# Attention output: the sum and its low-order half transposed together and added on VectorE, instead of folded by TensorE

## Chip, cores and metric

The kernel runs on one NeuronCore of one Trainium2 chip. The metric is the device time of one execution in microseconds (us); several runs of a program give a median. The trace is of one further, profiled execution.

## What is computed

One decoder layer over 2048 rows of width 1024 (float32). A projection feeds three groups: sparse attention (8 query heads on 2 key heads, the best 256 keys of each row chosen by an indexer), an S5 state-space scan, and attention into 256 memory rows (4 heads). Cut to what matters here:

```python
p = jax.nn.softmax(logits, axis=-1)                  # DSA attention, chosen keys
o = jnp.einsum('bqgrk,bqkgd->bqgrd', p, vg)
...
pm = jax.nn.softmax(sm, axis=-1)                     # memory attention
o_mem = jnp.einsum('bhlm,bmhd->blhd', pm, m_v)
...
cat = concat([o_att * silu(g_att), o_ssm * silu(g_ssm), o_mem * silu(g_mem)])
h = layer_norm(DN_ALPHA * x + cat @ w_out, ln_g, ln_b)
```

## The kernel before

Rows go in 16 tiles of 128. First comes the projection with the indexer's scores and the search for the 256 best keys; then attention (`attention`), 64 **units** of one row tile and one pair of heads; woven into it are the last gates, the projection and attention of the memory (`unit_mem`, 8 calls of two row tiles and 4 heads) and the scan (`stage_s5`); last the output projection and layer norm (`outputs`). Instructions are written in program order with named tiles. A scheduler then puts them into a fixed order on each engine by its own estimate, and adds semaphore waits where tiles are shared. On the chip TensorE (PE), VectorE (DVE), ScalarE (ACT) and GpSimd (POOL) each work strictly through their own order; SP issues all DMAs here, in its order too.

A unit has two parts. `att_qk` computes logits (L1116, L1117), adds the mask and takes the row maximum on VectorE (L1118), and ScalarE takes the exponential (L1123). `att_pv` transposes the weights on TensorE (L1140), splits them into a rounded part `hi` (ScalarE, L1144) and a rest `lo` (VectorE, L1145), and multiplies both with V into the sum `acc` in PSUM (L1147, L1148). V is kept as 128 columns, 64 of its rounded part beside 64 of its rest, so `acc` has 128 partitions: two halves of 64 that must still be added. That is done at the unit's end. ScalarE copies `acc` (128 x 256, two heads side by side) into `oT` (L1153). TensorE multiplies each head's 128 columns of `oT` by `ident2`, two identities of 64 stacked (L1156): this transposes and adds the halves at once, and the result `po` lies in the other half of `acc`'s bank. VectorE divides it by the softmax sum (`dn`, a reciprocal of L1151) and writes it back into `oT` (L1160), from where a DMA stores it (L1162). There is one `acc` and one `oT` buffer, so the next unit's first product (L1147) must wait until VectorE has read `po`.

`unit_mem` ends each of its 32 head-and-pair steps in the same way: `moT` (L1026), `ident2` (L1029), VectorE (L1031). A float32 product with `ident2` shows as two matmul instructions in the trace, so that both heads take four; a transpose shows as one.

Of the kernel before, what the change touches and what calls it, by code (L numbers as in the profile page):

```python
# [10 lines left out]
F32 = mybir.dt.float32  # L11
# [4 lines left out]
AF = mybir.ActivationFunctionType  # L16
OP = mybir.AluOpType
AX = mybir.AxisListType
# [69 lines left out]
class Layer:  # L88
# [82 lines left out]
    def rope(self, z, h, d, tabs, e=None):  # L171

        e = e or self.nc.gpsimd
        r = d // 4
        v = z.rearrange("p (h d) -> p h d", d=d)
        ab = self.s1.tile([128, 2, h, r], F32, name="rab", tag="o", bufs=1)
        a, b = ab[:, 0], ab[:, 1]
        cc = tabs[:, None, 0:r].broadcast_to([128, h, r])
        ss = tabs[:, None, r:2 * r].broadcast_to([128, h, r])
        e.tensor_tensor(a, v[:, :, 0:r], cc, op=OP.mult)  # L180
        e.tensor_tensor(b, v[:, :, 0:r], ss, op=OP.mult)
        hf = r // 2
        e.tensor_tensor(v[:, :, 0:hf], a[:, :, 0:hf], b[:, :, hf:r], op=OP.add)
        e.tensor_tensor(v[:, :, hf:r], a[:, :, hf:r], b[:, :, 0:hf], op=OP.add)
# [793 lines left out]
    def unit_mem(self, pp, MK, MV, sp, ps):  # L978

        nc = self.nc  # L980
        P = []
        dn = sp.tile([128, 2, 4], F32, name="mdn", bufs=2)
        for j in range(2):
            i = 2 * pp + j
            q = sp.tile([128, 256], F32, name="mq", bufs=2)
            nc.sync.dma_start(out=q, in_=self.QMD[i])
            st = sp.tile([128, 4, 2, 64], F32R, name="mst", bufs=2)
            self.split_heads(st, q)
            pt = ps.tile([128, 4, 128], F32R, name="fx", bufs=2)
            for h in range(4):  # L990
                nc.tensor.transpose(pt[:, h], st[:, h].rearrange("p a d -> p (a d)"), self.identr)
            qs = sp.tile([128, 4, 128], F32R, name="mqs", bufs=2)
            nc.scalar.activation(qs, pt.bitcast(F32), AF.Copy)
            mx = sp.tile([128, 2, 2], F32, name="mmx", bufs=2)
            p = sp.tile([128, 4, 256], F32, name="mP", bufs=4)
            for b in range(2):
                lg = ps.tile([128, 2, 256], F32, name="fx", bufs=2)
                for a in range(2):
                    nc.tensor.matmul(lg[:, a], qs[:, 2 * a + b], MK[:, a, b].rearrange("p a b -> p (a b)"),
                                     start=True, stop=False)  # L1000
                    nc.tensor.matmul(lg[:, a], qs[:, 2 * a + b], MK[:, a, 2 + b].rearrange("p a b -> p (a b)"),
                                     start=False, stop=True)
                nc.vector.tensor_reduce(mx[:, b], lg, axis=AX.X, op=OP.min)
                for a in range(2):
                    h = 2 * a + b
                    nc.scalar.activation(p[:, h], lg[:, a], AF.Exp, bias=mx[:, b, a:a + 1], scale=-1.0,
                                         accum_out=dn[:, j, h:h + 1])
            P.append(p)
        nc.vector.reciprocal(dn, dn)
        om = sp.tile([128, 2, 4, 64], F32, name="mom", bufs=2)  # L1010
        for h in range(4):
            pt = ps.tile([128, 2, 2, 128], F32, name="fx", bufs=2)
            for k in range(2):
                for j in range(2):
                    nc.tensor.transpose(pt[:, k, j], P[j][:, h, k * 128:(k + 1) * 128], self.ident)
            hi = sp.tile([128, 2, 256], F32R, name="mhi", bufs=2)
            lo = sp.tile([128, 2, 256], F32R, name="mlo", bufs=2)
            pf = pt.rearrange("p k j q -> p k (j q)")
            nc.scalar.activation(hi, pf, AF.Copy)
            nc.vector.tensor_tensor(lo, pf, hi.bitcast(F32), op=OP.subtract)  # L1020
            acc = ps.tile([128, 512], F32, name="fx", bufs=2)
            for k in range(2):
                nc.tensor.matmul(acc[:, 0:256], MV[:, k, h], hi[:, k], start=(k == 0), stop=False)
                nc.tensor.matmul(acc[:, 0:256], MV[:, k, h], lo[:, k], start=False, stop=(k == 1))
            oT = sp.tile([128, 256], F32, name="moT", bufs=2)
            nc.scalar.activation(oT, acc[:, 0:256], AF.Copy)  # L1026
            po = acc[:, 256:512]
            for j in range(2):
                nc.tensor.matmul(po[:, j * 64:(j + 1) * 64], oT[:, j * 128:(j + 1) * 128], self.ident2,  # L1029
                                 start=True, stop=True)  # L1030
            nc.vector.tensor_tensor(om[:, :, h], po[:, 0:128].rearrange("p (j d) -> p j d", d=64),  # L1031
                                    dn[:, :, h:h + 1].broadcast_to([128, 2, 64]), op=OP.mult)
        for j in range(2):
            nc.sync.dma_start(out=self.OMD[2 * pp + j], in_=om[:, j].rearrange("p a b -> p (a b)"))

# [91 lines left out]
    def att_pv(self, i, pr, pd, V, sp, ps):  # L1127

        nc = self.nc
        nk = i + 1  # L1130
        g = pr // 2
        dp, P = pd[0], pd[1:]
        acc = ps.tile([128, 512], F32, name="acc", bufs=1)
        for k0 in range(0, nk, 2):
            kw = min(2, nk - k0)
            self.npt += 1
            pt = ps.tile([128, 2, 2, 128], F32, name="pt", bufs=3)
            for k in range(kw):
                for hj in range(2):
                    nc.tensor.transpose(pt[:, k, hj], P[hj][:, (k0 + k) * 128:(k0 + k + 1) * 128], self.ident)  # L1140
            hi = sp.tile([128, 2, 256], F32R, name="hi", tag=f"h{self.npt % 3}", bufs=1)
            lo = sp.tile([128, 2, 256], F32R, name="lo", tag=f"h{self.npt % 3 + 3}", bufs=1)
            pf = pt.rearrange("p k j q -> p k (j q)")
            nc.scalar.activation(hi[:, :kw], pf[:, :kw], AF.Copy)  # L1144
            nc.vector.tensor_tensor(lo[:, :kw], pf[:, :kw], hi[:, :kw].bitcast(F32), op=OP.subtract)  # L1145
            for k in range(kw):
                nc.tensor.matmul(acc[:, 0:256], V[(k0 + k) // 4][:, (k0 + k) % 4, g], hi[:, k], start=(k0 + k == 0), stop=False)  # L1147
                nc.tensor.matmul(acc[:, 0:256], V[(k0 + k) // 4][:, (k0 + k) % 4, g], lo[:, k], start=False, stop=(k0 + k == nk - 1))  # L1148
            yield
        dn = sp.tile([128, 2], F32, name="dn", bufs=2)  # L1150
        nc.vector.reciprocal(dn, dp)  # L1151
        oT = sp.tile([128, 256], F32, name="oT", tag="o", bufs=1)
        nc.scalar.activation(oT, acc[:, 0:256], AF.Copy)  # L1153
        po = acc[:, 256:512]
        for hj in range(2):
            nc.tensor.matmul(po[:, hj * 64:(hj + 1) * 64], oT[:, hj * 128:(hj + 1) * 128], self.ident2,  # L1156
                             start=True, stop=True)
        oa = oT[:, 0:128]
        ov = oa.rearrange("p (j d) -> p j d", d=64)
        nc.vector.tensor_tensor(ov, po[:, 0:128].rearrange("p (j d) -> p j d", d=64),  # L1160
                                dn[:, :, None].broadcast_to([128, 2, 64]), op=OP.mult)
        nc.sync.dma_start(out=self.OAD[i][:, pr * 128:(pr + 1) * 128], in_=oa)  # L1162

    def attention(self, K, V, sp, ps, after=None):
# [13 lines left out]
        def ahead(j):  # L1178
            i, pr = work[j]
            if pr == 0:  # L1180
                st[i] = self.att_q(i, first[i] % 2, sp)
                while kv[0] <= max(t for t, _ in work[:j + 5]):
                    self.load_kv(kv[0], K, V, sp)
                    kv[0] += 1
            pd[j] = []
            return self.att_qk(i, pr, st[i], K, sp, ps, pd[j], j % 2)
        for _ in ahead(0):
            pass
        done = 0
        for j, w in enumerate(work):  # L1190
            a, na = iter(()), 0
            if j + 1 < len(work):
                a, na = ahead(j + 1), 2 * ((work[j + 1][0] + 4) // 4)
            nb = (w[0] + 2) // 2
            k = 0
# [218 lines left out]
```

## Time and profile before

| | |
|---|---|
| median of 3 runs | 1437.96 us (1436.89 to 1439.36) |
| profiled execution, its own time | 1432.55 us |
| its span | 1430.8 us |
| TensorE busy, share of the span | 94% |
| VectorE | 74% |
| ScalarE | 61% |
| GpSimd | 36% |
| granted TensorE clock, mean | 0.977 of full speed |

The span runs from the first to the last recorded instruction; 1.75 us of the execution lie around it. Matmuls overlap each other and their ends are modelled, so TensorE's busy time says more of where it waits than of how much it could do; the distance from the start of one group of its instructions to the start of the next is the better price. Stages lie one after another in the trace: projection and search to about 600 us, then attention with memory and scan to about 1240 us, then the output projection.

### The profile page before, as it was taken

The numbers are of one execution on the slowest core, as the hardware profiler recorded it, in microseconds if no ns is written. First come the engines' busy times: TensorE is split into PE (matmuls) and PEld (weight loads), VectorE is DVE, ScalarE is ACT, GpSimd is POOL, SyncE is SP. The second block draws the span as 40 slices with busy tenths as digits, with TensorE's granted clock in tenths as the row PEclk, the third lists the DMA queues.
The fourth block names the chain that finished last, engine by engine and source line by source line (L and its number), as shares of the span: only waits on it lengthen the run. The fifth ranks groups of instructions, "written<-read, shape, count | busy, mean of one in ns | idle before, by whom it ended". The sixth has DMA issues, their size and how long they took to land. (4 is left out here: it accounts for less than half of the span.)

```text
span 1430.8 us, 25169 instructions
## 1 busy us (share of the span) xinstructions
PE 1339.1 (94%) x8398; PEld 1181.4 (83%) x8398; DVE 1056.8 (74%) x2195; ACT 877.1 (61%) x1727; POOL 512.3 (36%) x1024
## 2 busy tenths in 40 slices
PE   7898999999869999999899999999899998999997
PEld 5687888988748988998798999998788886888885
DVE  4545785599875998865788888987788789565663
ACT  4575866775646854456788888877565677422221
POOL 1778443444993010023000000008786003254441
PEclk9799999999979999999999999999999999999998
DMA  9887454446545478552423011114112015465531
GB/s 344 264 308 239 166 170 164 169 157 214 181 136 195 138 256 299 184 168 78 125 69 94 25 59 43 36 45 115 51 42 64 25 60 185 133 224 177 177 133 62
DMA packets 128714, 206.58 MB, mean 144 GB/s; under 512 B 25088, under 2 KB 81792, under 8 KB 128320
## 3 DMA queue, kind: packets, MB, share of 16 engines
q1 hardware_dynamic: 128576, 204.89, 44.0%
q8 instruction: 68, 1.11, 0.3%
q14 instruction: 70, 0.57, 0.1%
HBM read 124.00 MB, written 77.10 MB: 141 GB/s over the span
## 5 line engine op out<-in xcount | busy, mean ns | idle before, releaser
L371 PE MATMUL fx<-whi,xhi 128*128 128x256 f32 (+3 forms) x912 | 307.1, 337 | 6.2 <-ACT xhi L139 2.5
L373 PE MATMUL fx<-whi,xlo 128*128 128x256 f32 (+3 forms) x912 | 305.7, 335 | 1.6 <-DMA xlo<-XD 1.6
L372 PE MATMUL fx<-wlo,xhi 128*128 128x256 f32 (+3 forms) x912 | 305.2, 335 | 0.0
L1145 DVE TENSOR_TENSOR lo<-pt,hi 128x512 fp32r<-128x512 f32 (+1 forms) x288 | 183.3, 654 | 48.3 <-ACT hi L1144 46.4
L453 DVE SCALAR_TENSOR_TENSOR sc<-rl,wsc,sc 128x1024 f32<-128x1024 f32 (+7 forms) x154 | 172.7, 1121 | 53.0 <-ACT rl L449 48.5
L371 PEld LDWEIGHTS fx<-whi,xhi 128*128 128x128 f32 x912 | 175.5, 192 | 24.0 <-ACT xhi L139 2.9
L1144 ACT ACTIVATE hi<-pt 128x512 fp32r<-128x512 f32 (+1 forms) x288 | 157.4, 578 | 59.6 <-PE pt L1140 29.9
L373 PEld LDWEIGHTS fx<-whi,xlo 128*128 128x128 f32 x912 | 175.4, 192 | 17.1 <-DMA xlo<-XD 2.0
L372 PEld LDWEIGHTS fx<-wlo,xhi 128*128 128x128 f32 x912 | 175.5, 192 | 15.4
L1123 ACT ACTIVATE S<-S,mx 128x1024 f32<-128x1024 f32 (+15 forms) x128 | 154.4, 1209 | 41.5 <-DVE mx L1118 39.3
L1140 PE MATMUL pt<-ident,S 128*128 128x128 f32 x1088 | 169.1, 276 | 9.4 <-DVE lo L1145 5.6
L449 ACT ACTIVATE rl<-pi 128x1024 f32<-128x1024 f32 (+7 forms) x176 | 140.1, 816 | 59.7 <-PE pi L442 42.1
L1148 PE MATMUL acc<-lo,V 128*128 128x256 f32 x544 | 144.3, 293 | 3.3 <-DVE lo L1145 3.1
L1140 PEld LDWEIGHTS pt<-ident,S 128*128 128x128 f32 x1088 | 128.4, 143 | 22.3 <-DVE lo L1145 6.9
L1147 PE MATMUL acc<-hi,V 128*128 128x256 f32 x544 | 145.2, 293 | 1.8 <-ACT hi L1144 1.4
L1116 PE MATMUL pl<-K,qs 128*128 128x512 f32 x320 | 133.7, 419 | 8.7 <-DVE mx L1118 8.4
L1118 DVE CUSTOM_DVE_ANT_0 S<-pl,mb,mx 128x512 f32<-128x512 f32 (+3 forms) x192 | 123.8, 645 | 17.6 <-PE pl L1117 13.6
L1117 PE MATMUL pl<-K,qs 128*128 128x512 f32 x320 | 117.6, 368 | 0.0
L1148 PEld LDWEIGHTS acc<-lo,V 128*128 128x128 f32 x544 | 103.5, 190 | 11.3 <-DVE lo L1145 7.6
L1147 PEld LDWEIGHTS acc<-hi,V 128*128 128x128 f32 x544 | 103.6, 190 | 6.7 <-ACT hi L1144 2.1
L442 PE MATMUL pi<-kidx,qst 128*128 128x512 f32 (+3 forms) x304 | 94.8, 390 | 15.2 <-ACT rl L449 14.6
L1118 DVE CUSTOM_DVE_ANT_0 S<-pl,mb 128x512 f32<-128x512 f32 (+3 forms) x128 | 80.7, 634 | 18.3 <-PE pl L1117 10.9
(351 smaller groups left out, 2881.2 us busy)
## 6 DMA issues: line engine op xcount, KB each, us to landing
xhi<-XD SPq DMA_DIRECT2D x32, 512.0 KB, 4.1
xlo<-XD SPq DMA_DIRECT2D x32, 512.0 KB, 5.1
QD<-kt SPq DMA_DIRECT2D x32, 256.0 KB, 2.5
qs<-QD SPq DMA_DIRECT2D x32, 256.0 KB, 3.0
xo<-x SPq DMA_DIRECT2D x16, 512.0 KB, 4.4
out<-xo SPq DMA_DIRECT2D x15, 512.0 KB, 2.7
raw<-xT SPq DMA_DIRECT2D x14, 512.0 KB, 5.4
XD<-xhi SPq DMA_DIRECT2D x14, 512.0 KB, 3.3
```

What stands on the lines that cost most here:

```text
L371: nc.tensor.matmul(p, x[0][:, k], w[0][:, k], start=(k == 0), stop=False)
L372: nc.tensor.matmul(p, x[0][:, k], w[1][:, k], start=False, stop=False)
L373: nc.tensor.matmul(p, x[1][:, k], w[0][:, k], start=False, stop=(k == KT - 1))
L449: nc.scalar.activation(rl[:, :cw], pi[:, :cw], AF.Relu)
L453: nc.vector.scalar_tensor_tensor(dst, rl[:, :cw], wsc[:, h:h + 1], dst, op0=OP.mult, op1=OP.add, accum_out=stt[:, 0, ch:ch + 1] if h == 7 ...
L1118: nc.vector.tensor_tensor_reduce(S[:, c0:c0 + cw], pl[:, :cw], mb[:, c0:c0 + cw], scale=-0.125, scalar=(3e38 if ci == 0 else mx[:, ci - 1: ...
L1123: nc.scalar.activation(S[:, :n], S[:, :n], AF.Exp, bias=mx[:, nch - 1:nch], scale=-1.0, accum_out=dp[:, hj:hj + 1])
L1140: nc.tensor.transpose(pt[:, k, hj], P[hj][:, (k0 + k) * 128:(k0 + k + 1) * 128], self.ident)
L1144: nc.scalar.activation(hi[:, :kw], pf[:, :kw], AF.Copy)
L1145: nc.vector.tensor_tensor(lo[:, :kw], pf[:, :kw], hi[:, :kw].bitcast(F32), op=OP.subtract)
L1147: nc.tensor.matmul(acc[:, 0:256], V[(k0 + k) // 4][:, (k0 + k) % 4, g], hi[:, k], start=(k0 + k == 0), stop=False)
L1148: nc.tensor.matmul(acc[:, 0:256], V[(k0 + k) // 4][:, (k0 + k) % 4, g], lo[:, k], start=False, stop=(k0 + k == nk - 1))
```

## The change

Both ends, of a unit and of a memory step, are rewritten in the same way. TensorE transposes each head's 128 columns of `oT` whole (two transposes for two heads, with `ident`); the result is 128 x 256, a row's two halves of 64 side by side for each head. VectorE adds the halves with one `tensor_reduce` that reads pairs 64 apart (256 numbers in, 128 out). GpSimd multiplies by `dn` in place, and the store follows that.

In attention `po` now takes `acc`'s own columns. `accs` holds two sums of 256 columns in one PSUM bank, used by turns, and `oT` has two buffers, `o0` and `o1`, used by turns. The scratch tile of `rope` moves from the name `o` to `o0`. Lines after 1028 move down by 1 to 4.

```diff
@@ rope
-        ab = self.s1.tile([128, 2, h, r], F32, name="rab", tag="o", bufs=1)
+        ab = self.s1.tile([128, 2, h, r], F32, name="rab", tag="o0", bufs=1)
@@ unit_mem
             for j in range(2):
-                nc.tensor.matmul(po[:, j * 64:(j + 1) * 64], oT[:, j * 128:(j + 1) * 128], self.ident2,
-                                 start=True, stop=True)
-            nc.vector.tensor_tensor(om[:, :, h], po[:, 0:128].rearrange("p (j d) -> p j d", d=64),
-                                    dn[:, :, h:h + 1].broadcast_to([128, 2, 64]), op=OP.mult)
+                js = slice(j * 128, (j + 1) * 128)
+                nc.tensor.transpose(po[:, js], oT[:, js], self.ident)
+            ov = om[:, :, h]
+            nc.vector.tensor_reduce(ov, po.rearrange("p (j a d) -> p j d a", j=2, a=2), axis=AX.X, op=OP.add)
+            nc.gpsimd.tensor_tensor(ov, ov, dn[:, :, h:h + 1].broadcast_to([128, 2, 64]), op=OP.mult)
@@ att_pv
-        acc = ps.tile([128, 512], F32, name="acc", bufs=1)
+        self.npair += 1
+        acc = self.accs[:, self.npair % 2]
...
-        oT = sp.tile([128, 256], F32, name="oT", tag="o", bufs=1)
-        nc.scalar.activation(oT, acc[:, 0:256], AF.Copy)
-        po = acc[:, 256:512]
+        oT = sp.tile([128, 256], F32, name="oT", tag=self.flip("o"), bufs=1)
+        nc.scalar.activation(oT, acc, AF.Copy)
+        po = acc
         for hj in range(2):
-            nc.tensor.matmul(po[:, hj * 64:(hj + 1) * 64], oT[:, hj * 128:(hj + 1) * 128], self.ident2,
-                             start=True, stop=True)
+            hs = slice(hj * 128, (hj + 1) * 128)
+            nc.tensor.transpose(po[:, hs], oT[:, hs], self.ident)
         oa = oT[:, 0:128]
         ov = oa.rearrange("p (j d) -> p j d", d=64)
-        nc.vector.tensor_tensor(ov, po[:, 0:128].rearrange("p (j d) -> p j d", d=64),
-                                dn[:, :, None].broadcast_to([128, 2, 64]), op=OP.mult)
+        nc.vector.tensor_reduce(ov, po.rearrange("p (j a d) -> p j d a", j=2, a=2), axis=AX.X, op=OP.add)
+        nc.gpsimd.tensor_tensor(ov, ov, dn[:, :, None].broadcast_to([128, 2, 64]), op=OP.mult)
@@ attention
+        self.accs, self.npair = ps.tile([128, 2, 256], F32, name="acc", bufs=1), 0
```

The scheduler draws a new order from the first unit's end on; up to there all five engines' orders agree but for a few rows. Two places matter.

**TensorE, from the end of one attention unit (row tile 12, second pair of heads) to the first product of the next.** In these rows a bracket names the engines whose semaphore ends the wait (DVE is VectorE, Activation is ScalarE). Before:

```order
L1156 MATMUL acc<-ident_75,oT 128x64
L1116 MATMUL pl<-K,qs 128x128 [waits DVE_49]
L1117 MATMUL pl<-K,qs 128x128
L1140 MATMUL pt<-ident,S 128x128 [waits DVE_49]
L1116 MATMUL pl<-K,qs 128x512 [waits DVE_49]
L1117 MATMUL pl<-K,qs 128x512
L1140 MATMUL pt<-ident,S 128x128 x3
L1140 MATMUL pt<-ident,S 128x128 [waits DVE_49,PE_49]
L1140 MATMUL pt<-ident,S 128x128 x3
L1140 MATMUL pt<-ident,S 128x128 [waits DVE_49,PE_49]
L1140 MATMUL pt<-ident,S 128x128 x3
L1147 MATMUL acc<-hi,V 128x256 [waits DVE_49,Activation_49]
```

The same place of the change:

```order
L1159 MATMUL acc<-ident,oT 128x128
L1117 MATMUL pl<-K,qs 128x128 [waits DVE_49]
L1118 MATMUL pl<-K,qs 128x128
L1117 MATMUL pl<-K,qs 128x512 [waits DVE_49]
L1118 MATMUL pl<-K,qs 128x512
L1142 MATMUL pt<-ident,S 128x128 [waits DVE_49,PE_49]
L1142 MATMUL pt<-ident,S 128x128 x3
L1142 MATMUL pt<-ident,S 128x128 [waits DVE_49,PE_49]
L1142 MATMUL pt<-ident,S 128x128 x3
L1142 MATMUL pt<-ident,S 128x128 [waits DVE_49,PE_49]
L1142 MATMUL pt<-ident,S 128x128 x3
L1149 MATMUL acc<-hi,V 128x256 [waits DVE_49,Activation_49]
```

The unit's end and the next unit's first product stand as far apart as they did, and the first product still waits for VectorE: the instruction that releases it is now the previous unit's `tensor_reduce` (L1162), as it was the previous unit's L1160. That holds for all 63 units that follow another.

**GpSimd, in the memory attention.** Before, these are only the splits of the memory queries (L961), two by two:

```order
L961 TENSOR_TENSOR mst<-mq,mst 128x2x64 [waits DMAHW3_49,PE_49,Activation_49]
L961 TENSOR_TENSOR mst<-mq,mst 128x2x64 [waits Activation_49]
L961 TENSOR_TENSOR mst<-mq,mst 128x2x64 [waits DMAHW4_49,PE_49,Activation_49]
L961 TENSOR_TENSOR mst<-mq,mst 128x2x64 [waits Activation_49]
L961 TENSOR_TENSOR mst<-mq,mst 128x2x64 [waits DMAHW6_49,PE_49,Activation_49]
```

Now the scalings of attention (L1163) and of the memory (L1033) stand between them, each waiting for VectorE:

```order
L1163 TENSOR_TENSOR oT<-oT,dn 128x128 [waits DMAHW0_49,DVE_49]
L1033 TENSOR_TENSOR mom<-mom,mdn 128x2x64 [waits DVE_49]
L1163 TENSOR_TENSOR oT<-oT,dn 128x128 [waits DMAHW1_49,DVE_49]
L1033 TENSOR_TENSOR mom<-mom,mdn 128x2x64 [waits DVE_49] x2
L1163 TENSOR_TENSOR oT<-oT,dn 128x128 [waits DMAHW5_49,DVE_49]
L961 TENSOR_TENSOR mst<-mq,mst 128x2x64 [waits DMAHW4_49,PE_49,Activation_49]
L961 TENSOR_TENSOR mst<-mq,mst 128x2x64 [waits Activation_49]
L1033 TENSOR_TENSOR mom<-mom,mdn 128x2x64 [waits DVE_49]
```

A split, and in the scan's stage a product of the scan, now stands behind scalings that wait for a unit's end.

## Rows read from the trace of the kernel before

**Rows 1.** The page's busy time, share and instructions of each engine.

```profile
PE 1339.1 (94%) x8398; PEld 1181.4 (83%) x8398; DVE 1056.8 (74%) x2195; ACT 877.1 (61%) x1727; POOL 512.3 (36%) x1024
```

**Rows 2.** Busy time by stretch: stretch, length, each engine's busy us, granted clock, DMA.

```profile
500.00:600.00 100.00, 99.45 (x625) 89.72 (x624) 92.52 (x161) 49.18 (x67) 10.95 (x24) 1.00 0.74 245
600.00:720.00 120.00, 112.01 (x794) 100.59 (x793) 76.22 (x201) 74.77 (x186) 22.75 (x28) 1.00 0.42 132
720.00:960.00 240.00, 236.79 (x1846) 221.52 (x1844) 205.81 (x562) 198.68 (x485) 11.78 (x29) 1.00 0.17 52
960.00:1240.00 280.00, 262.08 (x1761) 229.64 (x1760) 224.38 (x481) 185.95 (x319) 126.45 (x313) 0.98 0.26 74
1240.00:1431.00 191.00, 179.70 (x854) 149.52 (x852) 112.00 (x143) 48.08 (x76) 78.06 (x78) 0.98 0.49 164
```

**Rows 3.** The same view, of L1156 alone (PE, then weight loads).

```profile
600.00:720.00 120.00, 8.86 (x60) 8.11 (x60) 1.00 0.42 132
720.00:960.00 240.00, 18.55 (x128) 17.31 (x128) 1.00 0.17 52
960.00:1240.00 280.00, 9.74 (x68) 9.40 (x68) 0.98 0.26 74
```

**Rows 4.** The same view, of L1029 alone.

```profile
720.00:960.00 240.00, 17.56 (x124) 17.02 (x124) 1.00 0.17 52
960.00:1240.00 280.00, 0.55 (x4) 0.60 (x4) 0.98 0.26 74
```

**Rows 5.** TensorE in order of time: start us, us, instruction, count.

```profile
805.84 0.60 PE L1015 MATMUL fx<-ident,mP 128*128 128x128 f32 x4
806.28 0.56 PE L1156 MATMUL acc<-ident,oT 128*128 128x64 f32 x4
806.67 0.39 PE L1140 MATMUL pt<-ident,S 128*128 128x128 f32 x2
806.90 0.56 PE L1029 MATMUL fx<-ident,moT 128*128 128x64 f32 x4
807.29 0.61 PE L1140 MATMUL pt<-ident,S 128*128 128x128 f32 x4
807.65 0.36 PE L1147 MATMUL acc<-hi,V 128*128 128x256 f32 x1
```

**Rows 6.** VectorE's groups by shape: count, busy us, mean ns, idle before and releaser.

```profile
L1145 DVE TENSOR_TENSOR lo<-pt,hi 128x512 fp32r<-128x512 f32 x256 | 171.1, 684 | 42.1 <-ACT hi L1144 41.2
L1003 DVE TENSOR_REDUCE mmx<-fx 128x2 f32<-128x512 f32 x32 | 21.7, 682 | 1.7 <-PE fx L1001 1.5
L1160 DVE TENSOR_TENSOR oT<-acc,dn 128x128 f32<-128x128 f32 x64 | 18.1, 284 | 10.0 <-PE acc L1156 8.3 <-issue 0.9 <-ACT mhi L1019 0.3
L1145 DVE TENSOR_TENSOR lo<-pt,hi 128x256 fp32r<-128x256 f32 x32 | 13.2, 416 | 6.2 <-ACT hi L1144 5.2 <-PE acc L1147 0.9
L1031 DVE TENSOR_TENSOR mom<-fx,mdn 128x128 f32<-128x128 f32 x32 | 9.0, 282 | 1.9 <-PE fx L1029 1.9
```

**Rows 7.** The same view, GpSimd's products of 128x128 and ScalarE's copy into oT.

```profile
L961 POOL TENSOR_TENSOR mst<-mq,mst 128x128 fp32r<-128x128 f32 x32 | 14.1, 462 | 207.2 <-ACT mst L960 207.2
L180 POOL TENSOR_TENSOR rab<-zs,tab 128x128 f32<-128x128 f32 x16 | 12.7, 796 | 45.9 <-ACT zs L325 45.9
L1153 ACT ACTIVATE oT<-acc 128x256 f32<-128x256 f32 x64 | 25.0, 390 | 8.1 <-PE acc L1148 4.7 <-issue 1.2 <-DMA OAD<-oT 1.2
```

**Rows 8.** Who waited for whom, 960 to 1240 us: us in total, times, longest.

```profile
POOL BP L764 <- DMA OAD<-oT: 6.5, 1, 6.5
PE pl L1116 <- DVE mx L1118: 6.4, 4, 4.1
DVE tmp L787 <- POOL BP L766: 3.4, 2, 2.5
```

**Rows 9.** The same view, 600 to 1240 us.

```profile
PEld acc L1147 <- DVE oT L1160: 1.5, 4, 0.5
```

More of the change, by code (lines that the diff above doesn't have):

```diff
@@ L1146, in att_pv @@
             for k in range(kw):
-                nc.tensor.matmul(acc[:, 0:256], V[(k0 + k) // 4][:, (k0 + k) % 4, g], hi[:, k], start=(k0 + k == 0), stop=False)
-                nc.tensor.matmul(acc[:, 0:256], V[(k0 + k) // 4][:, (k0 + k) % 4, g], lo[:, k], start=False, stop=(k0 + k == nk - 1))
+                nc.tensor.matmul(acc, V[(k0 + k) // 4][:, (k0 + k) % 4, g], hi[:, k], start=(k0 + k == 0), stop=False)
+                nc.tensor.matmul(acc, V[(k0 + k) // 4][:, (k0 + k) % 4, g], lo[:, k], start=False, stop=(k0 + k == nk - 1))
             yield
```

## The prediction

> **What bounds the kernel now.** I read the page's busy line first [rows 1]: TensorE is busy for 94% of the span and VectorE for 74%. Such shares are averages, so the second view is the busy time by stretch [rows 2], cut where the work changes. The edited instructions run only from 600 to 1240 us [rows 3, 4]; before and after that nothing is edited. In that part the reader is to see two things. TensorE has the largest number in each stretch (112 of 120, 237 of 240, 262 of 280 us), so time taken off it can shorten the kernel. And VectorE comes close behind in the long middle stretch, 205.8 of 240 us or 86%, against 64% before it and 80% after it. GpSimd is nearly free in the middle, 11.8 of 240 us, and busy for 126 of 280 us where the scan runs.
>
> **What TensorE loses and gains.** Each end of a unit or of a memory step issues four matmul instructions, and the row order shows their price as the distance to the next start: 806.28 to 806.67 and 806.90 to 807.29, 0.39 us each [rows 5]. The counts are 256 instructions at L1156 and 128 at L1029 [rows 3, 4], so 64 and 32 ends: 15 in the first stretch, 32 + 31 = 63 in the middle, 17 + 1 = 18 in the last. The two transposes that replace them are of the kind that the kernel already does. Four took 0.44 us (from 805.84) and 0.36 us (from 807.29), two took 0.23 us (from 806.67) [rows 5]. I take 0.20 us for two, with ends of 0.18 and 0.23. Each end so frees 0.39 - 0.20 = 0.19 us of TensorE (0.16 to 0.21): 96 x 0.19 = 18.2 us, by stretch 2.9, 12.0 and 3.4 us.
>
> **What VectorE gains.** It gave 284 ns and 282 ns to the product it did here, 128 numbers out of PSUM [rows 6]. Now it reduces 256 numbers to 128. No row shows a reduction into pairs. The cheap end is 284 ns, as it writes the same 128 numbers; the dear end is 682 ns, the row of the one reduction in this stage, which reads 512 numbers [rows 6]. The nearest row by size is the 256-wide subtraction out of PSUM, 416 ns, and its 512-wide form takes 684 ns, as the 512-wide reduction does, so the number of elements read seems to set the time. I take 416 ns: 0.13 us more for each end, by stretch 2.0, 8.3 and 2.4 us.
>
> **How much of the freed time counts.** In the first stretch VectorE has 76 us of work in 120, so TensorE's 2.9 us count whole. In the middle VectorE would have 205.8 + 8.3 = 214.1 us of work in 240 - 12.0 = 228 us, or 94%. The best long stretch that this trace shows, the first of [rows 2], has 92.5 us in 100; held to that, 214.1 us need 231.5 us, so 8.5 of the 12.0 us count. In the last stretch VectorE has room (227 of 277 us), but TensorE idles there for 18 us, waiting for row maxima among others [rows 8], and shorter work turns partly into longer waiting: I count half, 1.7 us. Sum: 2.9 + 8.5 + 1.7 = 13.1 us.
>
> **Edits that I cost at nothing, with their cover.**
> - Scaling on GpSimd. The nearest product of the same size took 462 ns, one in smaller pieces 796 ns [rows 7]: 96 x 0.46 = 44 us, of which 29 fall into the middle stretch, where GpSimd works 12 of 240 us. Behind a scaling stand, on its own engine, the memory splits, the scan's products and the rounding of the output weights; on SP the store of `oT`, which now waits for GpSimd in place of VectorE, and all loads ordered behind it. No DMA is added. If that cover fails it is the second rival below.
> - Two sums in a bank. The order shows that the next unit's first product waits for the previous unit's reduction, as it waited for L1160, and with the same rows in between. Nothing is freed; TensorE's weight loads waited only 1.5 us in all for that [rows 9], which is the most it could give. The Trainium skill, "PSUM — Partial Sum Buffer", section on bank collisions, says to guard PSUM by bank and not by address, since two engines may not touch one bank at once even in different columns. By that rule two sums in one bank cannot run past each other and this edit gives 0; by addresses alone it would give up to the 1.5 us of that row. The waits in the changed order agree with the rule.
> - Two `oT` buffers. ScalarE waited 1.2 us for the store of `oT` [rows 7]; it is not the bound, so I count 0 (at most 1.2 us). Its copy keeps its size and its 390 ns.
> - `rope` takes another buffer name, long before attention.
> - The chain from the last product to the next unit's first one loses 0.19 us on TensorE and gains 0.13 us on VectorE, about even.
>
> **The number.** The profiled execution took 1432.55 us, so the same execution of the change should take 1419.5 us. The median of the runs, 1437.96 us, lies 5.4 us above the profiled execution; I carry that over and predict 1425 us. A measurement of this kernel can tell about 0.2%, or 2.9 us, from no change. The scheduler's new order also moves dozens of small waits by amounts that no row shows; I let that widen the range and not move the number.
>
> **Rivals.**
> 1. *All of it counts.* VectorE runs as densely as in its best 100 us and beyond, and the waits of the last stretch shrink as well. Then 18.2 us come off, or with the 1.5 and 1.2 us of the small edits 21 us: 1417 us; with transposes at their cheap end and part of the last stretch's idle time gone, 1413. For it: VectorE's waits in the middle are for ScalarE and TensorE. Against it: 94% of VectorE for 228 us stands nowhere in this trace.
> 2. *GpSimd's strict order (slower).* A scaling waits for its unit's reduction, and everything behind it on GpSimd waits too; in the scan's stage VectorE waits for GpSimd's BP (3.4 us, the longest 2.5) and GpSimd waited once for 6.5 us behind a store of `oT` on the DMA queue [rows 8]. Those 18 ends each add 0.46 us to an engine already working 126 of 280 us, and the wait for the reduction before it. If each puts 1.06 us into the scan's chain, and VectorE and TensorE stand at scan instructions in their own orders meanwhile, 18 x 1.06 = 19 us go, 6 more than the gain: 1444 us. It decides from 13.1 / 18 = 0.7 us for each end. Against it: TensorE's waits for GpSimd in this stretch are too small for the first rows of the view, and attention is there to fill.
> 3. *The reduction is dear.* If pairs cost more than elements, at 550 ns the middle has 205.8 + 63 x 0.27 = 222.8 us of VectorE work; at 92.5% that is 240.9 us, so nothing is gained there. The first and last stretch leave 4 us: 1434 us. At 682 ns it is 231 / 0.925 = 249.7 us, and the kernel is about 5 us slower: 1443 us. Against it: the two 512-wide rows agree within 2 ns [rows 6].
> 4. *The two sums do not run past each other*, so that part of the change does not do what its shape suggests. This is no case of its own: the order shows it, and the sum has it at 0.
>
> **Chances.** The forecast 0.42; rival 1 0.22; rival 2 0.20, of which 0.14 ends slower and 0.06 within the bound; rival 3 0.16, of which 0.08 faster, 0.05 within and 0.03 slower. Faster by more than 0.2%: 0.42 + 0.22 + 0.08 = 0.72. Within: 0.11. Slower: 0.17. The range runs from 1412, just under rival 1's end, to 1444, where rivals 2 and 3 end. The forecast's own range is 1418 to 1431.
>
> **What would show it.** In the changed profile: 192 transposes of 128x128 from `oT` and `moT` in place of 384 matmuls of 128x64, two of them about 0.20 us from start to start; `tensor_reduce` near 416 ns, at 550 or more rival 3 is right; GpSimd's scalings near 460 ns, and no wait of TensorE or VectorE for GpSimd that grew by more than a few us in the scan's stage, else rival 2; in the middle stretch VectorE's share up from 86% to over 90%, with the stretch some 8 us shorter. The first 600 us and the output stage should keep their lengths within 2 us. The prediction is wrong in its reasons if the attention part shrinks by the right amount while VectorE's share stays at 86%, or if the time comes from the first 600 us.

## The result and the profile after

The change takes 1418.28 us, the median of 4 runs (1416.98 to 1428.75), against 1437.43 us for the kernel before in the same comparison: a ratio of 0.990 with a 95% interval of 0.987 to 0.993. A second comparison on another occasion gave 0.9919 (0.9900 to 0.9939), by its medians 1422.36 against 1434.88 us. So the gain is 12 to 14 us by the ratios, and 12.5 and 19.2 us by the two pairs of medians. The profiled execution took 1419.1 us, its span is 1417.2 us and the mean granted TensorE clock 0.976, where it was 0.977.

First the busy time of the engines, which answers to [rows 1]:

```profile
PE 1319.8 (93%) x8206; PEld 1158.5 (82%) x8206; DVE 1060.2 (75%) x2195; ACT 874.7 (62%) x1727; POOL 546.1 (39%) x1120
```

There are 192 matmul instructions fewer and 96 GpSimd instructions more, as the edit says. Fixed windows as in [rows 2] would cut the changed kernel at other work, so the next two views cut both traces at the same events: the first unit's end, the first and the last memory end, the last unit's end, the end of the span. The columns are those of [rows 2]. Before:

```profile
619.00:722.70 103.70, 95.65 (x693) 85.77 (x692) 63.83 (x183) 68.63 (x176) 22.53 (x27) 1.00 0.36 112
722.70:962.80 240.10, 236.95 (x1844) 221.73 (x1843) 205.03 (x562) 198.87 (x483) 11.78 (x29) 1.00 0.17 51
962.80:1236.30 273.50, 255.58 (x1722) 223.96 (x1721) 222.77 (x477) 183.15 (x315) 126.00 (x313) 0.98 0.26 74
1236.30:1430.80 194.50, 183.40 (x872) 152.59 (x870) 112.30 (x144) 48.08 (x76) 78.51 (x79) 0.98 0.49 163
```

After:

```profile
615.60:718.10 102.50, 91.30 (x653) 80.66 (x653) 61.81 (x181) 66.43 (x173) 30.86 (x43) 1.00 0.36 107
718.10:946.10 228.00, 223.90 (x1711) 206.70 (x1710) 209.91 (x556) 198.69 (x485) 35.38 (x87) 1.00 0.19 57
946.10:1221.80 275.70, 255.64 (x1704) 222.34 (x1703) 224.74 (x484) 183.37 (x318) 129.34 (x335) 0.98 0.26 73
1221.80:1417.20 195.40, 183.35 (x871) 152.53 (x869) 108.08 (x144) 48.06 (x76) 79.80 (x80) 0.98 0.50 163
```

The middle stretch gives 12.1 us. The first gives 1.2 us, the last takes 2.2 us back. Part of that is moved work. These stretches hold 16, 63 and 17 ends, so 32, 126 and 34 instructions should be gone (two for each end), but 40, 133 and 18 are: some attention work now runs later. The output stage is 0.9 us longer, and the part before the first unit's end, whose order is the same but for a few rows, is 3.4 us shorter. Over the whole attention part, before and after:

```profile
619.20:1236.40 617.20, 588.08 (x4254) 531.40 (x4252) 491.42 (x1219) 450.65 (x972) 160.41 (x369) 0.99 0.24 72
615.90:1221.90 606.00, 570.64 (x4063) 509.63 (x4061) 496.16 (x1219) 448.49 (x972) 195.68 (x464) 0.99 0.25 73
```

TensorE is busy 17.4 us less, and the part is 11.2 us shorter: TensorE's idle time there grew from 29.1 to 35.4 us. By the stretches above (length less busy time) it grew from 8.1 to 11.2 us in the first, from 3.2 to 4.1 in the middle and from 17.9 to 20.1 in the last.

TensorE in order of time, at the place of [rows 5]:

```profile
805.11 0.38 PE L1159 MATMUL acc<-ident,oT 128*128 128x128 f32 x2
805.33 0.38 PE L1142 MATMUL pt<-ident,S 128*128 128x128 f32 x2
805.55 0.38 PE L1030 MATMUL fx<-ident,moT 128*128 128x128 f32 x2
805.76 0.60 PE L1142 MATMUL pt<-ident,S 128*128 128x128 f32 x4
```

Two transposes take 0.22 and 0.21 us from start to start, where four products took 0.39. The groups by shape, which answer to [rows 6, 7]:

```profile
L1162 DVE TENSOR_REDUCE oT<-acc 128x128 f32<-128x256 f32 x64 | 26.8, 418 | 11.7 <-PE acc L1159 9.4 <-ACT S L1124 1.6 <-issue 0.5
L1032 DVE TENSOR_REDUCE mom<-fx 128x128 f32<-128x256 f32 x32 | 13.3, 415 | 0.0
L1163 POOL TENSOR_TENSOR oT<-oT,dn 128x128 f32<-128x128 f32 x64 | 28.1, 439 | 243.9 <-DVE oT L1162 227.3 <-issue 6.8 <-DMA MK<-MKD 6.6
L1033 POOL TENSOR_TENSOR mom<-mom,mdn 128x128 f32<-128x128 f32 x32 | 12.9, 403 | 66.9 <-DVE mom L1032 66.3 <-PE acc L1149 0.5
L1155 ACT ACTIVATE oT<-acc 128x256 f32<-128x256 f32 x64 | 24.7, 386 | 8.6 <-PE acc L1150 4.8 <-issue 3.8
```

The reduction costs what the 256-wide subtraction costs. ScalarE's copy into `oT` waits no more for the store, which cost it 1.2 us in [rows 7]. Last, who waited for whom from 600 to 1240 us, beside [rows 8, 9]:

```profile
PE acc L1150 <- DVE lo L1147: 10.5, 6, 3.2
PE acc L1159 <- ACT oT L1155: 3.2, 4, 2.0
DVE tmp L787 <- POOL BP L766: 2.8, 2, 1.9
DVE dn L1153 <- POOL oT L1163: 2.6, 2, 2.5
PEld acc L1149 <- DVE oT L1162: 2.1, 5, 0.6
```

The rows of the kernel before that answer to the first two:

```profile
PE acc L1148 <- DVE lo L1145: 3.1, 6, 1.5
PE acc L1156 <- ACT oT L1153: 1.8, 3, 0.8
```

No engine waits much for the scaling: VectorE twice, 2.6 us in all. TensorE's wait for a split's rest (`lo`) before a product was 3.1 us and is 10.5 us. All six of these waits lie in the last stretch, where part of them stands in place of other waits: those for row maxima fell from 6.4 to 4.5 us there. In the first stretch TensorE waits longer for ScalarE's copy into `oT` (2.5 us, 1.0 before) and once, 1.8 us, for a load of `qs`. GpSimd's idle time in front of its scalings, 227 us, costs nothing; the engine is free then.

### The profile page after: what moved, and what is told of

Its sections match the earlier page's. It is cut to its first block, busy times and chain, and to the rows that moved or that the text cites. A ratio compares the mean times of both kernels' runs of the same rounds, so it can differ in the third digit from the quotient of the medians.

```text
span 1417.2 us, 24963 instructions
## 1 busy us (share of the span) xinstructions
PE 1319.8 (93%) x8206; PEld 1158.5 (82%) x8206; DVE 1060.2 (75%) x2195; ACT 874.7 (62%) x1727; POOL 546.1 (39%) x1120
## 4 chain that ended last, share of the span: by engine, by line
PE 61%; DVE 10%; POOL 10%; DMA 6%; issue 5%; ACT 4%; SPq 1%; POOLq 0%; DVEq 0%; ACTq 0%
PE fx L371 6%; PE fx L373 6%; PE fx L372 6%; PE pt L1142 6%; PE pl L1117 4%; PE acc L1150 3%; PE acc L1149 3%; PE pl L1118 3%; PE pi L442 2%; DVE sc L453 2%; PE pl L1266 2%; PE pl L1267 2%; PE pl L1265 2%; PE fx L1265 2%; PE fx L1267 2%
## 5 line engine op out<-in xcount | busy, mean ns | idle before, releaser
L1142 PE MATMUL pt<-ident,S 128*128 128x128 f32 x1088 | 165.2, 276 | 5.2 <-DVE lo L1147 4.2
L1150 PE MATMUL acc<-lo,V 128*128 128x256 f32 x544 | 144.1, 293 | 10.6 <-DVE lo L1147 10.5
L1163 POOL TENSOR_TENSOR oT<-oT,dn 128x128 f32<-128x128 f32 x64 | 28.1, 439 | 243.9 <-DVE oT L1162 227.3
L1150 PEld LDWEIGHTS acc<-lo,V 128*128 128x128 f32 x544 | 102.8, 189 | 19.2 <-DVE lo L1147 15.0
```

The source lines that it names most:

```text
L1150: nc.tensor.matmul(acc, V[(k0 + k) // 4][:, (k0 + k) % 4, g], lo[:, k], start=False, stop=(k0 + k == nk - 1))
```

## The experiments

The scheduler draws a new order for every kernel, so an edit never changes one thing alone: work also moves between stretches. Totals are therefore compared first, and stretches only where they hold the same work. Each run also gives its span and mean granted clock. In every trace here the granted clock of a stretch is 1.00 or 0.50, that is 2.4 or 1.2 GHz. At 0.50 at most half of the time is lost, so span x (1 - clock) is what these stretches cost at most; the table calls it half clock, and what is left of the span the rest, both in us. Means over the runs of a kernel, each ratio to before on the same occasion (runs 1 to 4 on one, 5 to 8 on the next, 9 to 12 on the third):

| kernel | median us | ratio to before (95%) | mean span | mean clock | half clock | rest |
|---|---|---|---|---|---|---|
| before, three occasions | 1433.4, 1434.9, 1436.1 | 1 | 1431.1, 1432.9, 1433.4 | 0.977, 0.976, 0.977 | 33, 34, 34 | 1398, 1399, 1400 |
| the change | 1422.36 | 0.9919 (0.9900 to 0.9939) | 1419.8 | 0.975 | 36 | 1384 |
| attention ends alone | 1424.87 | 0.9948 (0.9931 to 0.9966) | 1423.4 | 0.975 | 35 | 1388 |
| memory ends alone | 1428.07 | 0.9964 (0.9948 to 0.9979) | 1426.1 | 0.980 | 28 | 1398 |
| one sum, one `oT` | 1430.42 | 0.9988 (0.9976 to 1.0000) | 1428.4 | 0.973 | 38 | 1390 |
| two sums, one `oT` | 1430.88 | 0.9968 (0.9953 to 0.9982) | 1428.3 | 0.972 | 40 | 1388 |
| one sum, two `oT` | 1419.55 | 0.9905 (0.9885 to 0.9926) | 1418.2 | 0.976 | 33 | 1385 |
| scaling on VectorE | 1429.94 | 0.9982 (0.9968 to 0.9997) | 1428.0 | 0.973 | 38 | 1390 |
| transposes twice | 1439.25 | 1.0027 (1.0011 to 1.0044) | 1435.9 | 0.975 | 35 | 1401 |
| scaling twice | 1425.92 | 0.9940 (0.9914 to 0.9966) | 1424.5 | 0.973 | 38 | 1386 |
| reduction twice | 1455.78 | 1.0145 (1.0117 to 1.0174) | 1453.7 | 0.975 | 36 | 1417 |
| before with two `oT` | 1436.65 | 1.0007 (0.9987 to 1.0027) | 1434.7 | 0.975 | 35 | 1399 |
| own output tile | 1421.69 | 0.9922 (0.9894 to 0.9951) | 1420.8 | 0.975 | 35 | 1386 |

The clock of single runs of one kernel differs by up to 0.01, so a half-clock mean is known to some 2 us.

**1 and 2. The two ends apart.** The change with the memory's ends as before, and the kernel before with the memory's ends changed:

```diff
@@ unit_mem
...
-                nc.tensor.transpose(po[:, js], oT[:, js], self.ident)
...
+                nc.tensor.matmul(po[:, j * 64:(j + 1) * 64], oT[:, j * 128:(j + 1) * 128], self.ident2,
+                                 start=True, stop=True)
```

> Attention's unit ends as in the change (with its two sums and two oT buffers), the memory attention's 32 ends as before. My theory (the gain is TensorE time freed at each end, 0.19 us, counted where TensorE is the limit): 64 of 96 ends remain, so two thirds of the change's gain, about 0.6 to 0.7% faster than before. Rival (the gain is the scheduler's new order, or run noise): no relation to the number of ends, anything from 0 to 1.4%.

> The reverse: only the memory attention's 32 ends changed. Theory: 32 x 0.19 = 6 us, all of it in the middle stretch, about 0.4% faster than before; e1 and e2 together should make about the change's 1%. Rival (order or noise): no such sum.

They came out 8.5 and 5.3 us below before by their medians, and 0.52% and 0.36% by their ratios; together 0.88%, near the change's 0.8 to 1.0%. So both ends bring something, and the intervals have room for the 64 to 32 of their counts. The table adds a doubt on the second: its rest is that of before, and its gain is in the half-clock column, 28 against 33 us.

**3. One sum and one `oT` again, GpSimd kept.**

```diff
@@ att_pv
-        self.npair += 1
-        acc = self.accs[:, self.npair % 2]
+        acc = ps.tile([128, 256], F32, name="acc", bufs=1)
...
-        oT = sp.tile([128, 256], F32, name="oT", tag=self.flip("o"), bufs=1)
+        oT = sp.tile([128, 256], F32, name="oT", tag="o0", bufs=1)
```

> The change with one sum buffer and one oT buffer again. Theory: two sums in a bank free nothing, and the second oT buffer at most 1.2 us, so the same time as the change within 2 us. Rival (the buffers let units overlap): most of the gain over 10 us is lost, time back above 1428 us.

The ratio is 0.9988: 0.0069 of the span, 10 us, are lost. Two edits that the prediction had at nothing carry most of the gain between them. Runs 6 and 7 part them.

**4. Scaling on VectorE.** `nc.gpsimd.tensor_tensor` becomes `nc.vector.tensor_tensor` in both places.

> The change with the scaling on VectorE after the reduction, in place of GpSimd. It adds about 96 x 0.2 = 19 us of VectorE work, 13 of them in the middle stretch. Theory as predicted (VectorE near its densest in the middle stretch): about 8 to 13 us of the gain are lost there, 1427 to 1432 us. Rival (TensorE alone is the limit, VectorE has room): lost at most 3 us, under 1422 us.

About 9 us are lost, by the ratios. Where is the surprise. The middle stretch of this kernel, between its first and last memory end:

```profile
721.00:948.60 227.60, 223.46 (x1699) 204.56 (x1698) 218.34 (x615) 195.75 (x481) 11.77 (x29) 1.00 0.19 56
```

It is as long as in the change with the same TensorE work within 1%, while VectorE is busy 218.3 us of 227.6, 96%. So VectorE was not full at the change's 92%. The time went in the last stretch, which takes 284.9 us (948.6 to 1233.5) in place of 275.7. There TensorE is busy 4.8 us longer, with ten instructions more and a clock of 0.97 for 0.98, and idle 4.4 us longer; what in the new order did it is not shown. The scalings cost VectorE more than the 19 us expected, 25.0 us at L1163 and 9.0 at L1033, so about a quarter of their time came through.

**5. The change again**, beside the runs that follow.

> The change itself once more, as the base for the runs beside it. Theory and rival alike: about 1% faster than before, as in its first runs.

1422.36 us, as in the table; its span of 1416.6 us is that of the first profile within 1 us.

**6 and 7. The two edits apart**: two sums with one `oT`, and one sum with two.

> The change with its two sums but one oT buffer. New theory (e3 lost most of the gain because a single oT is held through the scaling and the store, so ScalarE's copy of the next sum waits): it loses 8 to 12 us against the change, as e3 did. Rival (two sums are what pays, though they share a bank): it stays within 3 us of the change. Rival (only the scheduler's draw): no pattern between this and the next run.

> The reverse: one sum, two oT buffers. New theory: within 3 us of the change, since the next unit's first product waits for the reduction either way. Rival (two sums pay): 8 to 12 us slower than the change.

One `oT` costs 8.5 us by the medians (7 by the ratios); one sum costs nothing, it was 2.8 us faster, with overlapping intervals. So the second `oT` is the edit that counts. Two sums in a bank are worth nothing that these runs can tell: with one `oT` they are 0.0020 ahead (run 6 against 3, on two occasions), with two 0.0014 behind, both with overlapping intervals. The waits of the kernel with two sums and one `oT`, 600 to 1240 us:

```profile
PE acc L1159 <- ACT oT L1155: 7.4, 9, 3.5
DVE dn L1153 <- POOL oT L1163: 6.2, 9, 2.5
ACT oT L1155 <- DMA OAD<-oT: 6.0, 7, 1.8
```

ScalarE waits again for the store that frees `oT`, 6.0 us where it was 1.2 us before the change, since the store now comes behind GpSimd; and TensorE's transposes wait for ScalarE's copy, 7.4 us against 3.2. That is the mechanism as these waits show it, but the waits alone are not the whole price. By the table about half of the loss is in the rest (1388 against 1384) and half in the clock (40 against 36 us). In the trace the whole attention part of this kernel:

```profile
616.80:1234.30 617.50, 579.90 (x4062) 514.73 (x4061) 500.91 (x1219) 450.37 (x972) 201.57 (x464) 0.98 0.24 71
```

With one instruction fewer TensorE is busy 9.3 us longer than in the change, at a clock of 0.98 for 0.99: 27 us of this part ran at 0.50, against 10 us in the change's. One such place, TensorE first in order of time (in brackets its idle time and the releaser), then in three windows with the columns of [rows 2]:

```profile
980.94 1.03 PE L1142 MATMUL pt<-ident,S 128*128 128x128 f32 x8
983.78 0.39 PE L1149 MATMUL acc<-hi,V 128*128 128x256 f32 x1 [1.80 <-DVE oT L1162]
984.00 0.28 PE L1150 MATMUL acc<-lo,V 128*128 128x256 f32 x1
...
986.33 0.41 PE L1149 MATMUL acc<-hi,V 128*128 128x256 f32 x1
```

```profile
983.00:985.00 2.00, 1.22 (x10) 1.22 (x11) 2.00 (x5) 0.50 (x2) 2.00 (x2) 1.00 0.86 190
985.00:995.00 10.00, 7.35 (x30) 6.59 (x30) 10.00 (x16) 2.88 (x6) 5.53 (x14) 0.50 0.02 7
995.00:1005.00 10.00, 9.18 (x55) 8.02 (x53) 6.08 (x13) 5.58 (x13) 8.35 (x32) 0.98 0.05 12
```

TensorE stood 1.80 us for a reduction; a little later the granted clock is 0.50 for some 10 us, with a further wait of 2.65 us for `lo` in it, and products of 0.28 us take 0.41. The Trainium skill, "TensorE: Matmul & The Clock Gate", section "HAM oscillation — how this bites in real kernels", tells of a kernel in which waits for DMA lower the clock, so that the work behind each wait pays a second time. The trace agrees in the pattern, but the wait here is for VectorE, and it is shorter than those. Not every such wait does it: in the change's attention part three waits of 1.79 to 2.05 us were followed by no fall, while the clock fell behind a wait of 3.1 us and one of 3.2 us, both for `lo`. The first of these two:

```profile
991.90:998.70 6.80, 6.04 (x22) 5.31 (x23) 6.54 (x17) 4.13 (x7) 0.95 (x6) 0.50 0.22 76
```

**8. The transposes twice**: the line `nc.tensor.transpose(...)` stands two times in both places, 96 times 0.20 to 0.22 us more of TensorE.

> The change with each of its 192 transposes issued twice in a row, 96 x 0.20 = 19 us more TensorE work. Theory (TensorE's time at these ends counts almost whole, as the change's own saving did): 13 to 19 us slower than the change, back at before's time. Rival (VectorE is the limit in the middle stretch, TensorE's time counts half): 5 to 10 us slower.

16.9 us above the change by the medians and 15.5 by the ratios, 1401 against 1384 in the rest and nothing in the clock. So TensorE's time counts by seven to nine tenths, as the doubled transposes cost 19 to 21 us. The middle stretch shows it too:

```profile
717.50:956.40 238.90, 235.35 (x1822) 218.25 (x1821) 208.97 (x554) 196.68 (x484) 35.49 (x87) 1.00 0.18 54
```

238.9 against 228.0 us: 10.9 us longer, of the 13 us that its 63 ends pay at 0.21 us each. It holds 111 TensorE instructions more where 126 were added, so some of the missing 2 us is work that moved out.

**9. The kernel before with two `oT`** and nothing else of the change but the name of `rope`'s scratch tile.

```diff
-        oT = sp.tile([128, 256], F32, name="oT", tag="o", bufs=1)
+        oT = sp.tile([128, 256], F32, name="oT", tag=self.flip("o"), bufs=1)
```

> The kernel before with two transposed buffers in the attention and nothing else of the change (VectorE still scales, 4 products an end, one sum). Theory A: a second buffer is worth something only because the scaling on GpSimd and the store behind it hold the transposed buffer longer; before, the scaling was on VectorE and ScalarE waited for the store 1.2 us in all, so this kernel is within 2 us of before. Theory B: the buffer is a gain by itself, some 8 us as with the sums (one against two in the change: 8.5 us), so that only some 7 us of the change's gain come from TensorE's shorter ends.

The ratio is 1.0007 (0.9987 to 1.0027): the buffer is no gain by itself. It is worth 7 to 8.5 us in the change (12 us with one sum, by the ratios of runs 3 and 7 on two occasions). The waits of run 6 name the reason: the scaling and the store behind it hold the buffer longer. So it is the cover of the GpSimd step, and not a part of TensorE's gain. No run has the scaling on VectorE with one `oT`, so that GpSimd, and not another part of the new end, makes the second buffer needed rests on those waits.

**10. The scaling twice on GpSimd**, into a spare tile, here in attention and likewise in the memory:

```diff
+        sx = sp.tile([128, 128], F32, name="sx", bufs=1)
+        nc.gpsimd.tensor_tensor(sx.rearrange("p (j d) -> p j d", d=64), ov, dn[:, :, None].broadcast_to([128, 2, 64]), op=OP.mult)
```

> The change with every scaling on GpSimd issued a second time into a spare tile (same operands, same duration): 96 times 0.40 us, 38 us more of GpSimd. Theory A: with two transposed buffers GpSimd's step is covered; it costs 0 to 3 us. Theory B: GpSimd's place in the chain still counts, so at least a third comes through, 12 us or more, and TensorE or VectorE show waits for the scaling.

The ratio is 0.9940 against 0.9919: 0.0021, 3 us, at the edge of what was given for a covered step, with overlapping intervals. Most of 38 us of GpSimd work is hidden with two buffers. What shows is VectorE at the reciprocal, whose two `dn` buffers GpSimd now frees later:

```profile
DVE dn L1155 <- POOL sx L1167: 3.5, 7, 0.8
```

**11. The reduction twice on VectorE**: the line `nc.vector.tensor_reduce(...)` stands two times in both places.

> The change with every reduction on VectorE issued twice (same operands, same result): 96 times 0.42 us, 40 us more of VectorE, of them 26 us in the middle stretch of 228 us, where VectorE is busy 92% already. Theory A: TensorE and VectorE are both near full there, so VectorE becomes the bound: 210 plus 26 is 236 us at 93% busy, 254 us, so 26 us more in the middle, and 0 to 8 us elsewhere; 22 to 34 us above the change. Theory B: VectorE still has room and only the end's chain grows: 5 to 12 us above the change.

The ratio is 1.0145: 32 us above the change, inside the 22 to 34 us, but not where it was expected. The middle stretch and the last one:

```profile
714.20:941.20 227.00, 215.03 (x1554) 187.88 (x1552) 208.32 (x572) 182.79 (x464) 35.12 (x86) 1.00 0.17 52
941.20:1259.80 318.60, 289.41 (x1934) 247.68 (x1933) 264.74 (x579) 209.65 (x357) 134.18 (x339) 0.99 0.23 67
```

The scheduler moved attention work out of the middle, 1554 TensorE instructions for 1711, so the middle kept its length and the last stretch grew by 43 us. That added VectorE time costs in this part is shown by the total, 32 of 40 us; where it becomes the bound is not, since the stretches hold other work.

**12. One sum, and the reduced result in a tile of its own**, so that `oT` is free right after its transposes.

```diff
-        oa = oT[:, 0:128]
+        oa = sp.tile([128, 128], F32, name="oa", bufs=2)
```

> The change with one sum in its bank (as in the run with one sum and two transposed buffers) and the reduced result in a small tile of its own, two of them, so that a transposed buffer is free as soon as its two transposes are done, before GpSimd's scaling and the store. Theory A: two transposed buffers hide the scaling and the store already; within 2 us of the change and of that run. Theory B: the buffers are still held too long now and then; 3 us or more faster than the change.

0.9922, as the change (0.9919). Freeing `oT` earlier buys nothing more; two buffers cover the step. No kernel here is measurably better than the change. The one with one sum and two `oT` is as fast and simpler.

## Why the prediction was right, and where its steps were not

The direction and the size held: 13.1 us were forecast for an equal execution, and the ratios give 14 and 12 us, the mean spans of the second occasion 13.1 (1432.9 and 1419.8). That it fits so closely is in part luck, because two errors of the sum cancel. In the profiled pair the middle stretch gave 3.6 us more than was counted and the other two together 5.6 us less, so the edited part gave 11 us; another 3.4 us came from the part before the first unit's end, which the change does not touch.

- **TensorE's price: right.** Two transposes take 0.21 to 0.22 us (0.20 taken, ends 0.18 to 0.23), and TensorE is busy 17.4 us less, where 18.2 us were counted. Doubled, the transposes cost 15.5 to 16.9 of 19 to 21 us.
- **VectorE's price: right.** The reduction takes 415 to 418 ns where 416 were taken. The rows of the 256- and 512-wide operations named the price, and rival 3 falls.
- **"held to that, 214.1 us need 231.5 us, so 8.5 of the 12.0 us count": wrong.** The middle stretch became 12.1 us shorter, at a VectorE share of 92%; of the 133 instructions gone from it 7 are moved work, by TensorE's busy time (13.1 us less, for 12.0 counted) about 1 us. The densest 100 us of the trace were taken as a limit, but were only what that work needed: with the scaling on VectorE the same stretch ran in 227.6 us at 96%. In this stretch TensorE is busy for 98 to 99% before and after, and its time counts nearly whole. So here it was rival 1's mechanism. That does not make VectorE's time free: the doubled reductions cost 32 of 40 us (run 11), and the scaling on VectorE about 9 of 34 us (run 4), both in the last stretch, to which work had moved. From which share of VectorE on it costs, no run shows.
- **"TensorE's 2.9 us count whole" in the first stretch, and "I count half, 1.7 us" in the last: wrong in the profiled execution**, 1.2 us and -2.2 us. In the first TensorE was busy 4.4 us less but idle 3.2 us more, for the copy into `oT` and for `qs`: shorter work that turned into longer waiting, which the prediction feared for the last stretch only. In the last TensorE was busy as long as before (255.6 us), since work moved there (18 instructions gone, not 34), which the sum by stretches left out, and idle 2.1 us longer. Taken together the two were to give 4.6 us and gave -1.0.
- **"Two `oT` buffers. ... I count 0 (at most 1.2 us)": wrong.** The bound was read from the kernel before, in which VectorE scaled. With the new end a single buffer is held longer, and the second one is worth 7 to 8.5 us (run 6 against 5), nothing in the kernel before (run 9). The sum came out because the change brings both: the step's cost and its cover. The sentence on GpSimd named the store that now waits for it, and did not follow the buffer back to ScalarE's copy and TensorE's transposes.
- **"Two sums in a bank. ... this edit gives 0": right** (run 7). The bank rule of the Trainium skill that the prediction named, in "PSUM — Partial Sum Buffer", section "PSUM bank collisions raise a hardware error", agrees: one sum is as fast as two.
- **Rival 2, GpSimd's order: did not come.** Scalings took 0.40 us (L1033) and 0.44 us (L1163) in the mean, where 0.46 was taken; the longest wait for one is 2.5 us. Even doubled they cost about 3 us, with two buffers.
- **"The first 600 us ... should keep their lengths within 2 us": not in this pair of traces.** The part up to the first unit's end took 619.2 and 615.9 us. It is no gain of the change: with the same order there, the profiled executions of the other kernels end it between 615.1 and 618.8 us. So 2 us was too narrow a mark for two single executions, and the profile of before happened to stand at the long end.
- **"The median of the runs ... lies 5.4 us above the profiled execution; I carry that over": wrong.** The profiled execution was forecast at 1419.5 us and took 1419.1, but this time the median lay 0.8 us below it. So the median of 1425 us was missed by 6.7 us on the first occasion and 2.6 on the second. A single profiled execution is no base for a shift of the median.

What stays open is how much of each difference is the edit and how much the scheduler's new order, which decides where TensorE waits and so where the clock falls. The kernel with the memory's ends alone shows it most: by its median 5.3 us faster, by its rest not faster at all.

## What to carry to other kernels

A step moved to an idle engine is free only while something else does not wait for the buffer that it holds; follow the buffer to its next writer, and price a second one with the new step in place and not with the old one. A density that a trace shows may be only what the work needed and not what the engine can do, so it is no cap. And where every edit redraws the order, compare totals over several runs, with the granted clock beside them, before stretches are read.

## What the runs showed of the hardware

- A `tensor_reduce` that adds pairs 64 apart out of PSUM goes by the numbers that it reads: 256 in and 128 out take 415 to 418 ns, a plain 256-wide subtraction 416 ns [rows 6].
- The price of TensorE's waits comes partly later. Over the runs of one kernel the clock differed from 0.972 to 0.978 and the span with it, 1426.8 to 1415.1 us (the first occasion of the change): 0.006 of the span is 8.5 us, of a difference of 11.7. On the second occasion 0.980 and 0.972 went with 1417.6 and 1421.5 us, so the clock is not all of it. In the attention part the mean clock of the profiled executions is 0.99 before and after, so it explains none of the change's gain there; by the table it explains about half of what the single `oT` costs.
- GpSimd's in-place product of 128x128 took 0.40 us, less than the 0.46 us of the row that the prediction used. The trace of before had a closer one, a float32 product of 128x128 with a broadcast column at 402 ns (L823). The first of attention's 64 took 2.37 us; no run says why.
